# A gate computed token block by token block, and a planner with other costs, in a two-block transformer kernel

## The chip, the cores and the metric

The kernel runs on one core of one Trainium2 chip. Its time is the device time of one execution in microseconds. Three runs of the kernel before took 1854.78, 1855.92 and 1857.61 us; the median is 1855.92 us.

## What is computed

Two blocks on x of 512 tokens by 1024 features, all in float32. The first has two layers; in each, after an attention mixer, comes this (reference, cut):

```python
for i in range(2):
    m = _even_mixer(x, ...) if i % 2 == 0 else _odd_mixer(x, ...)
    x = _layer_norm(DN_ALPHA * x + m, ln1_g[i], ln1_b[i])
    x = _layer_norm(DN_ALPHA * x + _sq_relu_mlp(x, w_up[i], w_down[i]), ln2_g[i], ln2_b[i])
    gate = jax.nn.sigmoid(x @ ple_w_gate[i] + ple_b_gate[i])
    x = x + gate * (p[i] @ ple_w_proj[i])
```

`ple_w_gate[i]` is 1024x1024, `ple_w_proj[i]` 256x1024. The even mixer is latent attention beside sliding-window attention, the odd one attention with forget gates. The second block is `h = rmsnorm(x) @ w_in`, gated linear attention beside a short convolution, an output product, `rmsnorm`, a SiLU feed-forward part and a last `rmsnorm`.

## The kernel before, in words

**Numbers and tiles.** Every float32 matrix is split into a high and a low part (ACT casts the high part, L273; DVE subtracts it for the low part, L284), and each product is three matmuls: high by high, high by low, low by high (L245). A stationary operand is 128x128; a moving one has up to 512 columns. The tokens are four blocks t of 128, the 1024 output columns two halves h of 512. So one half of one token block of the gate is 8 x 3 = 24 matmuls of 128x512, and the whole gate 8 x 24 = 192; the projection p @ w_proj is 8 x 6 = 48.

**Weights.** SP loads a raw unit of 128x1024 (512 KB; L314) into a buffer of the pool `af_t`, ACT casts it, DVE subtracts, and the parts lie in `ar_t`. The gate's weight is eight such units, ("ga", i, h, u) with h the column half and u = 0..3; the projection's is two, ("pr", i, h). A matrix held in one half serves all four token blocks, and its units come free after the last of them.

**From one stage to the next.** A token block of x lies with tokens on partitions; as an operand it is wanted transposed. `to_T` (L631) does this by eight 128x128 transposes on PE (L254, four to a PSUM bank), a cast per bank on ACT and a subtraction per bank on DVE. What stands ahead of it is a chain over four engines. After the MLP it is `ln_finish` (L685): ACT sums the block's halves (`half_sum`, L678), GpSimd makes the mean (L692), ACT squares with accumulation, DVE subtracts and multiplies by g (first of two 128x1024 `scalar_tensor_tensor`, L298), GpSimd makes 1/sqrt in two small steps (`rsqrt`, L621 and L622), DVE scales and adds b (the second). After the gate of layer 1 it is `rms_T` (L737): Square on ACT, two small GpSimd steps, two `scalar_tensor_tensor` of 128x512, then `to_T`.

**The gate** (L1605). First the 48 projection matmuls, whose results ACT copies to SBUF (`keep`). Then for h, for t: 24 matmuls, then `ev_` (L1612): DVE adds the bias, ACT takes the sigmoid, DVE multiplies by the projection and adds to x. When the second half of a block is done, `post` starts: `to_T` after layer 0's gate, `rms_T` after layer 1's. Since h is the outer loop, all four `post` chains start in the second pass.

**What sets the order.** The program is written by generators that yield what they need; `Core.run` (L431) advances the one whose next operation can begin first by a model of the engines' clocks, in which each operation has a cost: a matmul at L235 to L245, a DVE operation in `vcost` (L275), a small GpSimd step where it is issued (L621, L622, L692). The order so made is the fixed program of each engine, which the chip carries out in order. A cost therefore changes no work, only where it stands, and which buffer it gets.

Of the kernel before, what the change touches and what calls it, by code (L numbers as in the profile page):

```python
# [13 lines left out]
ALU = mybir.AluOpType  # L14
# [3 lines left out]
D = 1024  # L18
NB = 4
# [9 lines left out]
class Arena:  # L29


    def __init__(self, ap, n, grain=G):
        self.grain, self.n = grain, 0
        self.used, self.wt, self.rd, self.segs = [], [], [], []
        self.shut = False
        self.add(ap, n)
# [107 lines left out]
class Core:  # L144


    def __init__(self, nc, ar, af, sm, ps):
        self.nc, self.ar, self.af, self.ps = nc, ar, af, ps
        self.clk = dict(pe=0.0, act=0.0, dve=0.0, pool=0.0, dma=0.0)
        self.bw = [0.0] * 8  # L150
        self.br = [0.0] * 8
        self.bfree = [True] * 8
        self.byname = {}
        for x in (ar, af, sm):
            self.names(x)
        self.psname = ps.tensor.name
        self.streams = []
        self.table = None

    def names(self, a):  # L160
        for base, g, ap in a.segs:
            self.byname[ap.tensor.name] = (a, base, g * a.grain)
# [73 lines left out]
    def mm(self, out, lhsT, rhs, start, stop, more=False):  # L236
        n = self.size(rhs)
        slow = 4 if rhs.dtype == F32 else 1
        m = self.size(lhsT)
        if rhs.dtype == F32R:  # L240
            cost = max((n + 32) / 2.4, 109 * m / 128)
        else:
            cost = slow * max(n / 2.39, 107 * m / (256 if rhs.dtype == BF16 else 128))
        self.op("pe", cost, [lhsT, rhs], [out])
        self.nc.tensor.matmul(out, lhsT, rhs, start=start, stop=stop, **(dict(skip_group_check=True) if more else {}))  # L245
# [27 lines left out]
        self.nc.scalar.copy(out, src)  # L273

    def vcost(self, n, fast):  # L275
        return n * (0.53 if fast else 1.042) + (66 if fast else 157)

    def tt(self, out, a, b, op, eng="dve"):
        if eng == "pool":
# [274 lines left out]
def model_kernel(ctx: ExitStack, tc: tile.TileContext, a: dict, dbg=None):  # L554
# [14 lines left out]
    c = Core(nc, R, F, Arena(sm_t, NS, 4), ps_t)  # L569
    xb = [F.take(D, 0) for _ in range(NB)]  # L570
    xt = [b.ap for b in xb]
# [26 lines left out]
    mhalf = cp.tile([P, 4], F32, name="mhalf")  # L598
# [12 lines left out]
    def hs(h):  # L611
        return slice(h * 512, h * 512 + 512)
# [5 lines left out]

    def rsqrt(src, n, scale, eps):
        v, r = small(n), small(n)  # L620
        c.pool(165, [src], [v]).tensor_scalar(out=v, in0=src, scalar1=scale, scalar2=eps, op0=ALU.mult, op1=ALU.add)  # L621
        c.pool(465 + 160 * (n - 1), [v], [r]).tensor_tensor(out=r, in0=v, in1=mhalf[:, :n], op=ALU.pow)  # L622
        return r

    def dump(name):
# [61 lines left out]
    def ln_finish(t, st, g, b, ev):  # L687
        m, v = small(1), small(1)
        tmp = yield from c.alloc(F, D)
        z = yield from c.alloc(F, D)  # L690
        yield ("x", [st])
        c.pool(400, [st], [m]).tensor_scalar(out=m, in0=st[:, 0:1], scalar1=st[:, 1:2], scalar2=-1.0 / D, op0=ALU.add, op1=ALU.mult)  # L692
        yield ("x", [m])
        c.act(z.ap, xt[t], AF.Square, bias=m, accum_out=v)
        c.stt(tmp.ap, xt[t], m, g, ALU.add, ALU.mult)
        z.free()
        r = rsqrt(v, 1, 1.0 / D, EPS1)
        yield ("x", [r])
        c.stt(xt[t], tmp.ap, r, b, ALU.mult, ALU.add)
        tmp.free()  # L700
        yield from to_T(t, xt[t], A["x"], 8, ev)
# [35 lines left out]
    def rms_T(t, g, dst, ev):  # L737
        ss = small(1)
        y = yield from c.alloc(F, D)
        c.act(y.ap, xt[t], AF.Square, accum_out=ss)  # L740
        r = rsqrt(ss, 1, 1.0 / D, EPS2)
        for h in range(2):
            c.stt(y.ap[:, hs(h)], xt[t][:, hs(h)], r, g[:, hs(h)], ALU.mult, ALU.mult)
        yield from to_T(t, y.ap, dst, 8, ev)
        y.free()

# [867 lines left out]
    def gate(i, pT, post):  # L1614
# [24 lines left out]
        def keep(b, z):  # L1639
            yield ("x", [c.pb(b)])  # L1640
            c.acopy(z.ap, c.pb(b))
            c.give(b)

        bps = {}
        for h in range(2):
            for t in range(NB):
                z = bps[h, t] = yield from c.alloc(F, 512)
                b = yield from tm(xcols(pT["x"], range(2), t), [("pr", i, h)], 512, [pT["ev"][t]], t == 3)
                c.spawn(keep(b, z), 0)
        for h in range(2):  # L1650
            keys = [("ga", i, h, u) for u in range(4)]
            for t in range(NB):
                bb = yield from tm(xcols(A["x"], range(8), t), keys, 512, [old[t]], t == 3)
                c.spawn(ev_(bb, bps[h, t], t, h), 0)
        for z in pT["b"]:
# [691 lines left out]
    def main():  # L2347
        yield from new_A()
        for t in range(NB):
            c.spawn(to_T(t, xt[t], A["x"], 8, A["ev"][t]), 0)  # L2350
        W.cap = 4
        yield from layer1()
        yield from mlp(0, pT := {})
        yield from gate(0, pT, lambda t, e: to_T(t, xt[t], A["x"], 8, e))
        W.cap = 4
        yield from layer2()
        yield from mlp(1, pT := {})
        n1 = yield from bcast(a["norm1_g_2"], D)
        yield from gate(1, pT, lambda t, e: rms_T(t, n1.ap, A["x"], e))
        W.cap = 5  # L2360

        def later(ev):
            yield ("x", list(ev))
            n1.free()

        c.spawn(later(A["ev"]), 0)
        yield from layer3()
        yield from ffn()
# [116 lines left out]
```

## Time and profile before

| | |
|---|---|
| profiled execution | 1856.44 us |
| span of its trace | 1854.7 us, so 1.74 us lie outside it |
| median of the runs | 1855.92 us |
| PE (matmuls) busy | 1815.6 us, 98% |
| DVE busy | 1169.7 us, 63% |
| ACT busy | 902.7 us, 49% |
| GpSimd (POOL) busy | 134.2 us, 7% |
| granted TensorE clock, mean of the span | 0.992 |

Read it by PE: 1854.7 less 1815.6 is 39.1 us in which PE does no matmul, in a few places; anywhere else a shorter step on another engine moves nothing. Granted clock is a share of full speed: 1.0 is 2.4 GHz, 0.5 is 1.2 GHz, and a figure between them is a stretch that was partly at each.

### The profile page before, as it was taken

What the parts mean: (1) busy time and instruction counts of PE and PEld (TensorE: products, weight loads), DVE (VectorE), ACT (ScalarE), POOL (GpSimd) and SP (SyncE); (2) the same over time, 40 slices, a digit from 0 to 9 for tenths busy, and PEclk for the clock granted to TensorE, in tenths of its full rate; (3) what the DMA queues carried; (4) which work ended last, traced back from release to release, by engine and by line L of the source; (5) the groups of instructions that cost most, each with busy time, mean ns of one, the idle gap of its engine ahead of it and who ended that gap; (6) DMA issues with size and microseconds to landing.
All of it is one profiled execution on the core that took longest, in us unless ns stands there. A gap on an engine that the chain in (4) does not pass through costs nothing. (4 is left out here: it accounts for less than half of the span.)

```text
span 1854.7 us, 23845 instructions
## 1 busy us (share of the span) xinstructions
PE 1815.6 (98%) x9096; PEld 1518.9 (82%) x9096; DVE 1169.7 (63%) x1947; ACT 902.7 (49%) x1594; POOL 134.2 (7%) x227
## 2 busy tenths in 40 slices
PE   8999999999998999999999999989999999999997
PEld 7876788888887888878888888878889898888886
DVE  4667667566568578778675656675675554644646
ACT  4567464545456365555645454563543243423434
POOL 1000011001011000000110010110010000100001
PEclk9999999999999999999999999999999999999999
DMA  5211256464562122323564736531222443633614
GB/s 171 82 36 47 91 182 163 105 188 85 176 151 89 46 92 69 114 69 114 171 159 112 192 71 193 126 109 65 69 91 75 141 172 103 158 124 80 171 23 97
DMA packets 63539, 212.01 MB, mean 114 GB/s; under 512 B 7544, under 2 KB 10160, under 8 KB 63424
## 3 DMA queue, kind: packets, MB, share of 16 engines
q1 hardware_dynamic: 50752, 165.39, 25.9%
q0 software_dynamic: 12672, 45.09, 14.0%
q8 instruction: 71, 1.16, 0.3%
q14 instruction: 44, 0.36, 0.1%
HBM read 208.32 MB, written 2.14 MB: 113 GB/s over the span
## 5 line engine op out<-in xcount | busy, mean ns | idle before, releaser
L245 PE MATMUL ps_t<-ar_t 128*128 128x512 f32 (+4 forms) x6591 | 1385.6, 367 | 9.4 <-DVE ar_t L293 3.3
L245 PEld LDWEIGHTS ps_t<-ar_t 128*128 128x128 f32 x6591 | 1140.7, 190 | 207.6 <-ACT ar_t L273 7.4
L284 DVE TENSOR_TENSOR ar_t<-af_t,ar_t 128x1024 fp32r<-128x1024 f32 (+5 forms) x456 | 467.5, 1043 | 365.0 <-ACT ar_t L273 361.4
L273 ACT CAST ar_t<-af_t 128x1024 fp32r<-128x1024 f32 (+5 forms) x467 | 412.2, 900 | 495.0 <-PE ps_t L245 325.8
L245 PE MATMUL ps_t<-ar_t,ax_r 128*128 128x512 f32 (+1 forms) x1050 | 258.2, 390 | 2.7 <-ACT ar_t L273 1.8
L245 PEld LDWEIGHTS ps_t<-ar_t,ax_r 128*128 128x128 f32 x1050 | 196.4, 190 | 43.6 <-ACT ar_t L273 2.2
L284 DVE TENSOR_TENSOR ar_t<-ps_t,ar_t 128x512 fp32r<-128x512 f32 (+3 forms) x207 | 117.0, 595 | 94.1 <-ACT ar_t L273 93.3
L273 ACT CAST ar_t<-ps_t 128x512 fp32r<-128x512 f32 (+3 forms) x207 | 98.8, 519 | 139.8 <-PE ps_t L254 70.0
L298 DVE SCALAR_TENSOR_TENSOR af_t<-af_t,ps_t 128x512 f32<-128x512 f32 (+2 forms) x218 | 138.2, 658 | 44.7 <-PE ps_t L245 38.7
L269 ACT ACTIVATE af_t<-af_t 128x512 f32<-128x512 f32 (+3 forms) x144 | 92.3, 644 | 103.9 <-DVE af_t L298 57.1
L284 DVE TENSOR_TENSOR ax_r<-af_t,ax_r 128x256 fp32r<-128x256 f32 (+5 forms) x119 | 91.7, 771 | 59.9 <-ACT ax_r L273 59.3
L273 ACT CAST ax_r<-af_t 128x256 fp32r<-128x256 f32 (+5 forms) x119 | 81.3, 687 | 81.4 <-PE ps_t L245 42.9
L284 DVE TENSOR_TENSOR af_t<-af_t 128x256 f32<-128x256 f32 (+2 forms) x228 | 99.5, 467 | 11.2 <-ACT af_t L269 8.4
L322 POOL DMA_DIRECT2D af_t<-in_w_down x64 | 55.5, 868 | 550.4 <-DVE ar_t L284 525.3
L254 PE MATMUL ps_t<-ident,af_t 128*128 128x128 f32 (+1 forms) x499 | 70.5, 279 | 14.1 <-DVE af_t L298 13.9
L273 ACT COPY af_t<-ps_t 128x512 f32<-128x512 f32 (+3 forms) x108 | 59.1, 569 | 46.6 <-PE ps_t L245 32.6
L254 PEld LDWEIGHTS ps_t<-ident,af_t 128*128 128x128 f32 (+1 forms) x499 | 59.4, 142 | 22.0 <-DVE af_t L298 15.7
L269 ACT ACTIVATE af_t<-af_t,sm_t 128x256 f32<-128x256 f32 (+4 forms) x92 | 60.6, 660 | 30.3 <-DVE sm_t L808 20.9
L245 PE MATMUL ps_t<-ax_r,ar_t 128*128 128x512 f32 (+4 forms) x343 | 70.3, 346 | 0.0
L298 DVE SCALAR_TENSOR_TENSOR af_t<-af_t,sm_t 128x1024 f32<-128x1024 f32 (+1 forms) x48 | 52.1, 1103 | 25.6 <-POOL sm_t L622 12.0
L269 ACT ACTIVATE af_t<-ps_t 128x512 f32<-128x512 f32 (+3 forms) x111 | 58.7, 529 | 15.5 <-PE ps_t L245 15.4
L245 PEld LDWEIGHTS ps_t<-ax_r,ar_t 128*128 128x128 f32 (+1 forms) x343 | 56.6, 186 | 8.3
(98 smaller groups left out, 670.1 us busy)
## 6 DMA issues: line engine op xcount, KB each, us to landing
af_t<-in_w_up SPq DMA_DIRECT2D x64, 512.0 KB, 6.0
af_t<-in_w_down POOLq DMA_DIRECT2D x64, 512.0 KB, 5.6
af_t<-in_w_down SPq DMA_DIRECT2D x48, 512.0 KB, 4.8
af_t<-in_w_ffn_gate SPq DMA_DIRECT2D x22, 512.0 KB, 4.5
af_t<-in_w_ffn_up SPq DMA_DIRECT2D x22, 512.0 KB, 4.5
af_t<-in_w_ffn_down POOLq DMA_DIRECT2D x20, 512.0 KB, 5.5
af_t<-in_ple_w_gate SPq DMA_DIRECT2D x16, 512.0 KB, 5.9
af_t<-in_w_ffn_down SPq DMA_DIRECT2D x15, 512.0 KB, 3.4
```

Source lines behind the costliest of these rows:

```text
L245: self.nc.tensor.matmul(out, lhsT, rhs, start=start, stop=stop, **(dict(skip_group_check=True) if more else {}))
L254: self.nc.tensor.transpose(out, src, ident)
L269: self.nc.scalar.activation(out, src, func, **kw)
L273: self.nc.scalar.copy(out, src)
L284: self.nc.vector.tensor_tensor(out, a, b, op=op)
L298: self.nc.vector.scalar_tensor_tensor(out, a, s, b, op0=op0, op1=op1)
L322: self.nc.gpsimd.dma_start(out, src, accum_op=ALU.add)
```

## The change

The planner's costs become three attributes (`tiny`, `two`, `edge`) that have one value while layer 0's attention (`layer1`) is recorded and another from there on. Against before, the small GpSimd steps cost 165 (which was 400 in `ln_finish`) and 465 in the first part and 850 and 1050 after it; a matmul's 32 extra columns and a DVE operation's 157 count as 0 and 66 in the first part and as before after it. `rms_T` issues one `scalar_tensor_tensor` of 128x1024 in place of two of 128x512. The gate's loops change places: t outside, h inside. So all eight weight units are needed within the first token block, and stay until the last; a block's `post` can start when its own two halves are done.

```diff
--- before.py
+++ after.py
@@ -156,6 +156,7 @@
         self.psname = ps.tensor.name
         self.streams = []
         self.table = None
+        self.tiny, self.two, self.edge = (165, 465), 66, 0
 
     def names(self, a):
         for base, g, ap in a.segs:
@@ -238,7 +239,7 @@
         slow = 4 if rhs.dtype == F32 else 1
         m = self.size(lhsT)
         if rhs.dtype == F32R:
-            cost = max((n + 32) / 2.4, 109 * m / 128)
+            cost = max((n + self.edge) / 2.4, 107 * m / 128)
         else:
             cost = slow * max(n / 2.39, 107 * m / (256 if rhs.dtype == BF16 else 128))
         self.op("pe", cost, [lhsT, rhs], [out])
@@ -273,7 +274,7 @@
         self.nc.scalar.copy(out, src)
 
     def vcost(self, n, fast):
-        return n * (0.53 if fast else 1.042) + (66 if fast else 157)
+        return n * (0.53 if fast else 1.042) + (66 if fast else self.two)
 
     def tt(self, out, a, b, op, eng="dve"):
         if eng == "pool":
@@ -618,8 +619,8 @@
 
     def rsqrt(src, n, scale, eps):
         v, r = small(n), small(n)
-        c.pool(165, [src], [v]).tensor_scalar(out=v, in0=src, scalar1=scale, scalar2=eps, op0=ALU.mult, op1=ALU.add)
-        c.pool(465 + 160 * (n - 1), [v], [r]).tensor_tensor(out=r, in0=v, in1=mhalf[:, :n], op=ALU.pow)
+        c.pool(c.tiny[0], [src], [v]).tensor_scalar(out=v, in0=src, scalar1=scale, scalar2=eps, op0=ALU.mult, op1=ALU.add)
+        c.pool(c.tiny[1] + 160 * (n - 1), [v], [r]).tensor_tensor(out=r, in0=v, in1=mhalf[:, :n], op=ALU.pow)
         return r
 
     def dump(name):
@@ -689,7 +690,7 @@
         tmp = yield from c.alloc(F, D)
         z = yield from c.alloc(F, D)
         yield ("x", [st])
-        c.pool(400, [st], [m]).tensor_scalar(out=m, in0=st[:, 0:1], scalar1=st[:, 1:2], scalar2=-1.0 / D, op0=ALU.add, op1=ALU.mult)
+        c.pool(c.tiny[0], [st], [m]).tensor_scalar(out=m, in0=st[:, 0:1], scalar1=st[:, 1:2], scalar2=-1.0 / D, op0=ALU.add, op1=ALU.mult)
         yield ("x", [m])
         c.act(z.ap, xt[t], AF.Square, bias=m, accum_out=v)
         c.stt(tmp.ap, xt[t], m, g, ALU.add, ALU.mult)
@@ -739,8 +740,7 @@
         y = yield from c.alloc(F, D)
         c.act(y.ap, xt[t], AF.Square, accum_out=ss)
         r = rsqrt(ss, 1, 1.0 / D, EPS2)
-        for h in range(2):
-            c.stt(y.ap[:, hs(h)], xt[t][:, hs(h)], r, g[:, hs(h)], ALU.mult, ALU.mult)
+        c.stt(y.ap, xt[t], r, g, ALU.mult, ALU.mult)
         yield from to_T(t, y.ap, dst, 8, ev)
         y.free()
 
@@ -1647,9 +1647,9 @@
                 z = bps[h, t] = yield from c.alloc(F, 512)
                 b = yield from tm(xcols(pT["x"], range(2), t), [("pr", i, h)], 512, [pT["ev"][t]], t == 3)
                 c.spawn(keep(b, z), 0)
-        for h in range(2):
-            keys = [("ga", i, h, u) for u in range(4)]
-            for t in range(NB):
+        for t in range(NB):
+            for h in range(2):
+                keys = [("ga", i, h, u) for u in range(4)]
                 bb = yield from tm(xcols(A["x"], range(8), t), keys, 512, [old[t]], t == 3)
                 c.spawn(ev_(bb, bps[h, t], t, h), 0)
         for z in pT["b"]:
@@ -2350,6 +2350,7 @@
             c.spawn(to_T(t, xt[t], A["x"], 8, A["ev"][t]), 0)
         W.cap = 4
         yield from layer1()
+        c.tiny, c.two, c.edge = (850, 1050), 157, 32
         yield from mlp(0, pT := {})
         yield from gate(0, pT, lambda t, e: to_T(t, xt[t], A["x"], 8, e))
         W.cap = 4
```

The same instructions are issued as before but for `rms_T`. PE's, DVE's and ACT's order differs in layer 0's attention, in the norm after it, at the end of each MLP with the gate behind it, in the norm after the second attention, and at the beginning and the end of the second block's mixer; inside the MLPs, the second attention, the feed-forward part and the end it is the same. On SP the fifth of the last six gate-weight loads moves ahead of the load of the gate's bias, so that seven of eight stand ahead of it and one behind (six and two before), in both layers.

**PE, end of the first MLP.** The transposes with `ident,af_t ... x8` are T(0) to T(3) of the norm after the MLP. Before:

```order
L245 MATMUL ps_t<-ar_t,ax_r 128x512 x45
L254 MATMUL ps_t<-ident,af_t 128x128 x8
L245 MATMUL ps_t<-ar_t,ax_r 128x512 x15
L254 MATMUL ps_t<-ident,af_t 128x128 x8
L245 MATMUL ps_t<-ar_t,ax_r 128x512 x12
L245 MATMUL ps_t<-ar_t 128x512 x18
L254 MATMUL ps_t<-ident,af_t 128x128 x8
L245 MATMUL ps_t<-ar_t 128x512 x24
L254 MATMUL ps_t<-ident,af_t 128x128 x8
```

Now:

```order
L246 MATMUL ps_t<-ar_t,ax_r 128x512 x13
L255 MATMUL ps_t<-ident,af_t 128x128 x8
L246 MATMUL ps_t<-ar_t,ax_r 128x512 x18
L255 MATMUL ps_t<-ident,af_t 128x128 x8
L246 MATMUL ps_t<-ar_t,ax_r 128x512 x30
L255 MATMUL ps_t<-ident,af_t 128x128 x8
L246 MATMUL ps_t<-ar_t,ax_r 128x512 x12
L246 MATMUL ps_t<-ar_t 128x512 x6
L255 MATMUL ps_t<-ident,af_t 128x128 x8
```

Counting the `ar_t,ax_r` and `ar_t` rows ahead together, T(0) stands 15 matmuls later in the program than it did, and there are 18, 30 and 18 matmuls between the four, where there were 15, 30 and 24. The second MLP's end has the same steps.

**DVE, the same place.** A `af_t,sm_t 128x1024` is a step of `ln_finish`: the first two are block 0's, the next two block 1's. `ar_t<-af_t,ar_t` is the low part of a weight unit, `ps_t 128x512` an addition of the MLP's product to the sum. Before:

```order
L298 SCALAR_TENSOR_TENSOR af_t<-af_t,ps_t 128x512
L298 SCALAR_TENSOR_TENSOR af_t<-af_t,sm_t 128x1024
L298 SCALAR_TENSOR_TENSOR af_t<-af_t,ps_t 128x512
L284 TENSOR_TENSOR ar_t<-af_t,ar_t 128x1024
L298 SCALAR_TENSOR_TENSOR af_t<-af_t,sm_t 128x1024 x2
L298 SCALAR_TENSOR_TENSOR af_t<-af_t,ps_t 128x512 x2
L298 SCALAR_TENSOR_TENSOR af_t<-af_t,sm_t 128x1024
L284 TENSOR_TENSOR ar_t<-ps_t,ar_t 128x4x128 x2
```

Now:

```order
L299 SCALAR_TENSOR_TENSOR af_t<-af_t,ps_t 128x512
L285 TENSOR_TENSOR ar_t<-af_t,ar_t 128x1024
L299 SCALAR_TENSOR_TENSOR af_t<-af_t,sm_t 128x1024
L299 SCALAR_TENSOR_TENSOR af_t<-af_t,ps_t 128x512
L285 TENSOR_TENSOR ar_t<-af_t,ar_t 128x1024
L299 SCALAR_TENSOR_TENSOR af_t<-af_t,ps_t 128x512 x2
L299 SCALAR_TENSOR_TENSOR af_t<-af_t,sm_t 128x1024 x2
L299 SCALAR_TENSOR_TENSOR af_t<-af_t,ps_t 128x512 x3
L299 SCALAR_TENSOR_TENSOR af_t<-af_t,sm_t 128x1024
L285 TENSOR_TENSOR ar_t<-ps_t,ar_t 128x4x128 x2
```

Between block 0's first and second step there stood one addition and one weight unit; now there stand one addition, a weight unit and two more additions, and another weight unit stands ahead of the first.

**PE, end of the gate of layer 1.** The rows with 128x272 are the first product of the second block, 24 for each token block, and need `rms_T` of that block. Before:

```order
L245 MATMUL ps_t<-ar_t 128x512 x30
L254 MATMUL ps_t<-ident,af_t 128x128 x8
L245 MATMUL ps_t<-ar_t 128x512 x12
L245 MATMUL ps_t<-ar_t 128x272 x18
L245 MATMUL ps_t<-ax_r,ar_t 128x272 x6
L245 MATMUL ps_t<-ar_t 128x272 x18
L254 MATMUL ps_t<-ident,af_t 128x128 x4
L245 MATMUL ps_t<-ax_r,ar_t 128x272 x6
L254 MATMUL ps_t<-ident,af_t 128x128 x12
L245 MATMUL ps_t<-ar_t 128x272 x18
L245 MATMUL ps_t<-ax_r,ar_t 128x272 x6
L245 MATMUL ps_t<-ar_t 128x272 x18
```

Now:

```order
L255 MATMUL ps_t<-ident,af_t 128x128 x8
L246 MATMUL ps_t<-ar_t 128x512 x42
L246 MATMUL ps_t<-ar_t 128x272 x6
L255 MATMUL ps_t<-ident,af_t 128x128 x8
L246 MATMUL ps_t<-ar_t 128x272 x12
L246 MATMUL ps_t<-ax_r,ar_t 128x272 x6
L246 MATMUL ps_t<-ar_t 128x272 x18
L246 MATMUL ps_t<-ax_r,ar_t 128x272 x6
L246 MATMUL ps_t<-ar_t 128x272 x18
L246 MATMUL ps_t<-ax_r,ar_t 128x272 x6
L255 MATMUL ps_t<-ident,af_t 128x128 x8
L246 MATMUL ps_t<-ar_t 128x272 x18
```

In the order of before T(3) is the last eight of the row of twelve transposes (the four rows ahead of them and the four further up are T(2)), and stands behind 18 + 6 + 18 + 6 = 48 matmuls of 128x272. Now T(0) has gone ahead into the gate, T(1) and T(2) stand at the top, and T(3) stands behind 6 + 12 + 6 + 18 + 6 + 18 + 6 = 72 of them.

## Rows read from the trace of the kernel before

**Rows 1.** The page's first part: busy us, share of the span, instructions

```profile
PE 1815.6 (98%) x9096; PEld 1518.9 (82%) x9096; DVE 1169.7 (63%) x1947; ACT 902.7 (49%) x1594; POOL 134.2 (7%) x227
```

**Rows 2.** Timeline of PE, first gate's start: start, us, work, idle before

```profile
564.08 1.09 PE L254 MATMUL ps_t<-ident,af_t 128*128 128x128 f32 x8 [3.02 <-DVE af_t L298]
564.92 3.68 PE L245 MATMUL ps_t<-ar_t,ax_r 128*128 128x512 f32 x15
...
574.07 0.50 PE L245 MATMUL ps_t<-ar_t 128*128 128x512 f32 x1 [1.85 <-ACT ar_t L273]
575.33 3.15 PE L245 MATMUL ps_t<-ar_t 128*128 128x512 f32 x8 [0.76 <-DVE ar_t L284]
```

**Rows 3.** Timeline of PE at the second gate's start

```profile
1217.42 1.65 PE L254 MATMUL ps_t<-ident,af_t 128*128 128x128 f32 x8 [2.85 <-DVE af_t L298]
...
1228.98 0.50 PE L245 MATMUL ps_t<-ar_t,ax_r 128*128 128x512 f32 x1 [1.78 <-ACT ar_t L273]
1230.24 4.04 PE L245 MATMUL ps_t<-ar_t,ax_r 128*128 128x512 f32 x11 [0.76 <-DVE ar_t L284]
```

**Rows 4.** Windows: length; busy of PE, PEld, DVE, ACT, POOL; clock; DMA

```profile
564.00:570.00 6.00, 5.92 (x34) 5.14 (x35) 6.00 (x10) 2.95 (x8) 1.51 (x2) 1.00 0.00 0
...
576.00:582.00 6.00, 6.00 (x25) 4.86 (x24) 4.62 (x5) 4.35 (x9) 0.59 (x2) 0.72 0.00 0
1218.00:1224.00 6.00, 6.00 (x27) 5.05 (x26) 5.74 (x9) 1.90 (x4) 1.16 (x2) 0.73 0.00 0
...
1230.00:1236.00 6.00, 5.76 (x19) 4.56 (x20) 5.18 (x6) 3.76 (x7) 0.27 (x1) 0.72 0.12 42
...
1302.00:1308.00 6.00, 6.00 (x34) 6.00 (x33) 2.76 (x5) 1.17 (x2) 0.00 (x0) 0.62 0.00 0
```

**Rows 5.** Timeline of DVE at the first gate's start

```profile
562.74 2.48 DVE L298 SCALAR_TENSOR_TENSOR af_t<-af_t,sm_t 128x1024 f32<-128x1024 f32 x2
565.14 1.27 DVE L298 SCALAR_TENSOR_TENSOR af_t<-af_t,ps_t 128x512 f32<-128x512 f32 x2
...
586.39 1.22 DVE L284 TENSOR_TENSOR ar_t<-af_t,ar_t 128x1024 fp32r<-128x1024 f32 x1 [0.20 <-ACT ar_t L273]
```

**Rows 6.** Timeline of SP: the last two loads of the first gate's weight

```profile
587.64 1.76 SPq L314 DMA_DIRECT2D af_t<-in_ple_w_gate  x2
```

**Rows 7.** The page's last part, loads: KB each, median us to landing

```profile
af_t<-in_ple_w_gate SPq DMA_DIRECT2D x16, 512.0 KB, 5.9
```

**Rows 8.** Timeline of POOL in the first gate's norm

```profile
564.31 0.96 POOL L621 TENSOR_SCALAR sm_t<-sm_t 128x1 f32<-128x1 f32 x1 [1.36 <-ACT af_t L269]
```

**Rows 9.** Timeline of PE at the second gate's end

```profile
1292.04 0.91 PE L245 MATMUL ps_t<-ax_r,ar_t 128*128 128x272 f32 x6
...
1295.04 0.60 PE L254 MATMUL ps_t<-ident,af_t 128*128 128x128 f32 x4
...
1301.60 1.97 PE L254 MATMUL ps_t<-ident,af_t 128*128 128x128 f32 x8 [4.77 <-DVE af_t L298]
```

**Rows 10.** Timeline of DVE there

```profile
1292.34 1.42 DVE L298 SCALAR_TENSOR_TENSOR af_t<-af_t,sm_t 128x512 f32<-128x512 f32 x2 [2.19 <-POOL sm_t L622]
...
1294.13 0.69 DVE L284 TENSOR_TENSOR af_t<-ps_t,af_t 128x512 f32<-128x512 f32 x1
...
1300.80 1.42 DVE L298 SCALAR_TENSOR_TENSOR af_t<-af_t,sm_t 128x512 f32<-128x512 f32 x2 [2.13 <-POOL sm_t L622]
```

**Rows 11.** Timeline of PE in the norm after layer 0's attention

```profile
236.40 2.29 PE L245 MATMUL ps_t<-ar_t 128*128 128x256 f32 x17 [1.24 <-DVE ar_t L284]
```

**Rows 12.** Timeline of PE in the norm after the second attention

```profile
890.14 1.09 PE L254 MATMUL ps_t<-ident,af_t 128*128 128x128 f32 x8 [1.50 <-DVE af_t L298]
```

**Rows 13.** Timeline of PE early in layer 0's attention

```profile
24.62 1.10 PE L245 MATMUL ps_t<-af_t,ax_f 128*128 128x512 f32 x2 [1.09 <-DMA af_t<-ed]
```

**Rows 14.** Timeline of PE and DVE where layer 0's query products begin

```profile
74.99 0.55 PE L254 MATMUL ps_t<-ident,af_t 128*128 128x128 f32 x3 [1.80 <-DVE af_t L298]
...
77.03 1.23 DVE L284 TENSOR_TENSOR ar_t<-af_t,ar_t 128x1024 fp32r<-128x1024 f32 x1 [0.27 <-ACT ar_t L273]
```

## The prediction

> **What bounds the kernel now.** The first part of the page comes first: PE is busy for 1815.6 us of the span [rows 1], and no other engine comes near. PE carries out its program in order, so the time is PE's work and the holes in it; DVE, ACT and GpSimd matter only where PE stands at an instruction whose operand is late. The list of what PE waited for leads to the places, and the timeline of PE shows each of them.
>
> At the start of the first gate PE reaches T(0) of the norm too early: it waits 3.02 us for DVE's last step, and later 1.85 and 0.76 us for the projection's weight, whose cast and subtraction stand late [rows 2]. In the stretch from 576 to 582 us the granted clock is 0.72 of 2.4 GHz, so part of it runs at 1.2 GHz [rows 4]; 0.28 x 6 = 1.7 us go there. Together 7.3 us. The second gate's start repeats it: 2.85, 1.78 and 0.76 us [rows 3], and two stretches at 0.73 and 0.72 [rows 4], 3.3 us: 8.7 us. At the second gate's end PE waits 4.77 us at T(3) [rows 9], and the stretch behind it has a clock of 0.62 [rows 4], 2.3 us more: 7.1 us. These three are 23.1 us. The norm after layer 0's attention has one wait of 1.24 us [rows 11], the one after the second attention 1.50 [rows 12], layer 0's attention 1.09 for a transfer [rows 13] and 1.80 at a transpose [rows 14]. The rest of PE's idle time, at the very start, at the end and in the second attention, lies where the order is the same.
>
> **The change part by part, in order of size.**
>
> Second gate's end. In the program of before the last product of the gate is followed by 48 matmuls of 128x272 and then T(3). Twenty-four of these take 3.0 us (1292.04 to 1295.04) [rows 9], so one takes 0.125, and the gate's last product ended 18 x 0.125 = 2.25 us ahead of the row at 1292.04, at 1289.8. Its addition on DVE came only at 1294.13, because the scaling of block 2 stood ahead and waited for GpSimd until 1292.34 [rows 10]: all four chains ran in the gate's second pass, close behind each other. In the new order a block's chain starts 48 matmuls after the one before, not 24, and those of blocks 0 to 2 are done before block 3's product ends. From the addition at 1294.13 to the scaling step at 1300.80 is 6.67 us, and one step of 128x1024 takes 1.24 (two take 2.48) [rows 5] where the two of 128x512 took 1.42. With the addition at 1290.0 it is done at 1290.0 + 6.7 + 1.2 = 1297.9. PE was at T(3) at 1301.60 - 4.77 = 1296.8 and now has 24 more matmuls ahead of it, so arrives at 1299.8. The wait goes, and so does the slow stretch behind it. What is late next is the product of block 3 itself, which now comes straight behind T(3) where another block's product lay between: one cast and one subtraction of a 128x512 tile, near 0.6 us each by DVE's 1.27 for two [rows 5]. I take 1.2 us for it. Gain 7.1 - 1.2 = 5.9; bounds 7.1, and 3.0 if the chain is no faster than before and only the 24 matmuls help.
>
> The merged scaling step costs DVE less, but T can no longer begin on its first half: 0.6 us later, in the margin of 1.9 us.
>
> Here the Trainium skill bears (GPSIMD Engine Reference, section Key points): GpSimd shares its SBUF interfaces with VectorE, and DVE instructions with two SBUF inputs contend with it. The trace agrees: one small step took 0.96 us beside a double-length DVE step [rows 8]. By the rule the longer scaling step holds a neighbour's small steps back by up to 0.6 us more; where no margin is left that is 0.6 us less gain, and since the blocks now lie 48 matmuls apart, the sum by the rule and mine are the same to 0.6.
>
> Second gate's start. T(0) stands 15 matmuls later, and 15 such matmuls take at most 3.68 us [rows 2]; I take 3.6. But on DVE one weight unit, the projection's (1.22), and two additions (1.27) [rows 5] have come between the first and the second step of block 0's norm, 2.5 us. The wait is 2.85 + 2.5 - 3.6 = 1.75 us in place of 2.85. The two waits for the projection's weight go, since this unit is what has come forward. For that the gate's units are late next: eight are wanted within the first block's 48 matmuls, 11.5 us at 3.6 / 15 = 0.24 each, where four were wanted there and four in the second pass, and DVE is already busy for all of 564 to 570 us [rows 4]. Eight by 1.22 is 9.8 us of DVE; several have been done by the time PE comes, and I take 0.5 us of small waits. The clock: it stayed at 1.00 behind the wait of 3.02 us and fell behind that of 2.85 [rows 2 to 4], so I count one stretch at half weight, 0.85 us. Left 1.75 + 0.5 + 0.85 = 3.1 of 8.7: gain 5.6, bounds 0 and 8.7.
>
> [...]
>
> First gate's start. The same steps: 3.02 + 2.5 - 3.6 = 1.9, with 0.5 and 0.85 makes 3.25 of 7.3: gain 4.1, bounds 0 and 7.3. Its end has no wait in either order, since T there waits for no norm.
>
> Norm after layer 0's attention. T(1) stands 6 matmuls earlier, and its two subtractions on DVE earlier with it, so the low parts that PE waited 1.24 us for are there: gain 1.2, bounds 0 and 1.2. In the norm after the second attention the wait of 1.50 us [rows 12] moves to the next product: nothing, bounds 0 and 1.5.
>
> Layer 0's attention. Six matmuls and two groups of transposes now stand ahead of the one that waits 1.09 us for a transfer [rows 13]: gain 1.0. Where the query products begin, the low part of a value-weight unit, 1.23 us [rows 14], comes ahead of the latent's low parts on DVE, and PE already stands there: loss 1.3. Net loss 0.3; bounds 2.9 better (both waits of rows 13 and 14 gone) and 2.5 worse (two such units).
>
> Second block's mixer and the norm behind it. No wait there before; the new order puts the norm's steps ahead of a feed-forward weight unit. I take one unit late, 1.2 us; bounds 0 and 2.5.
>
> The sum: 5.9 + 5.6 + 4.1 + 1.2 - 0.3 - 1.2 = 15.3 us. The profiled execution took 1856.44 us (the span and 1.74 us outside it), so 1841.1; it lay 0.5 above the median of the runs, so the forecast is **1841 us** (0.1 between the two is nothing). Its own range is 1834 to 1847.
>
> **The rivals.**
>
> *The gate starts keep their loss.* DVE is the second bound there: it was busy for the whole of 564 to 570 us [rows 4], and the new order asks more of it earlier. If the waits of T(0) only turn into waits for the gate's units, the 9.7 us of both starts stay and 15.3 - 9.7 = 5.6 is left: 1850.8. For it: a unit serves 6 matmuls, 1.44 us, and costs DVE 1.22, which leaves almost no room for the norm's own steps. Against: several units are subtracted before PE is there. Chance 0.20.
>
> *All of it.* T(0) is on time, no unit is late, the clock stays up: 3.1 + 3.25 more, 1834.8. For it: the same places lost nothing else before. Against: the sum of DVE's rows. Chance 0.15.
>
> *Slower: the eighth unit.* Two loads of the gate's weight were issued only at 587.64 us [rows 6], when buffers came free, and 5.9 us is a usual landing [rows 7]; in the new order one of them is still behind the bias load and is needed at the end of the first block, not in the second pass. Issued at 587.64 it is landed at 593.5 and, with a cast and a subtraction of about 1.2 us each, ready at 596. PE is done waiting at T(0) at 561.1 + 3.6 + 1.9 = 566.6, and has 102 matmuls and four groups of transposes at 0.84 (564.08 to 564.92) [rows 2] until it wants it: 566.6 + 24.5 + 3.4 = 594.5, so it would be 1.5 us late. It decides when it slips by a whole buffer turn: the gain of 15.3 is gone when both gates lose 7.7 us to it, and a slip of 10 us each gives 1841 + 20 = 1861. For it: nothing lets SP pass a waiting load. Against: its buffer is freed by the second unit, which is split early. Chance 0.06.
>
> *Near nothing.* Both starts keep their loss, layer 0 loses 2.5 instead of 0.3 and the mixer 2.5 instead of 1.2: 1850.8 + 3.5 = 1854.3. Chance 0.09.
>
> **How the numbers follow.** The forecast has 0.50. The range reaches from all of it with layer 0 better, 1832, to the gate starts keeping their loss with one more unit late, 1852; outside lie near nothing, slower, and a little at the lower end, under 0.2. Within 0.2% (3.7 us, about what a measurement of this kernel can tell from no change) is near nothing, 0.09; slower 0.06; faster 0.85.
>
> **What would show it.** In the new profile T(3) at the second gate's end begins without a wait and the clock stays at 1.00 there; T(0) at each start still waits for DVE, some 2 us, and no wait for the cast of the projection's weight is left; small waits for DVE stand in the gate's first 48 matmuls and none in the later ones; the wait of 1.24 us is gone; layer 0 is as long as before to 2 us. I am wrong in the gates if waits of several us for a weight's load or subtraction stand in the first block, and in layer 0 or the mixer if the stretches 0 to 230 or 1290 to 1510 us of before take over 3 us more.

## The result and the profile after

The changed kernel takes 1842.74 us (median of 4 runs, 1841.28 to 1842.99), the kernel before 1856.57 (4 runs); the ratio is 0.9925, with a 95% interval of 0.9908 to 0.9942. It is 13.8 us faster; forecast were 1841 us and a gain of 15.3, with a range of 1832 to 1852. The profiled execution took 1841.28 us, its span is 1839.6 us; it is the fastest of the four, 1.5 us under the median, so the places below add up to 15.1 us and not to 13.8. The page's first part [rows 1]:

```profile
PE 1810.7 (98%) x9096; PEld 1514.0 (82%) x9096; DVE 1165.8 (63%) x1939; ACT 901.0 (49%) x1594; POOL 141.3 (8%) x227
```
and the main lines of what PE waited for (us in total, times, longest), two of before and then those of the changed kernel:

```profile
PE ps_t L254 <- DVE af_t L298: 13.9, 5, 4.8
PE ps_t L245 <- ACT ar_t L273: 4.8, 4, 1.9
```
```profile
PE ps_t L255 <- DVE af_t L299: 6.9, 3, 3.0
...
PE ps_t L246 <- DVE ar_t L285: 3.1, 5, 0.8
PE ps_t L246 <- ACT ar_t L274: 2.6, 4, 1.1
...
PE ps_t L246 <- DMA af_t<-ed: 0.5, 1, 0.5
```

PE was idle for 28.9 us of the span (1839.6 less 1810.7), 39.1 before, and busy for 4.9 us less with the same matmuls, at a mean clock of 0.996 in place of 0.992. The waits for DVE's steps at L299 (L298 before) have gone from 13.9 us in five to 6.9 in three, those for a cast on ACT from 4.8 to 2.6. Where the difference was made is read at points that both programs pass with the same work behind them:

| the same point in both programs | before | after | ahead by |
|---|---|---|---|
| a product in layer 0's attention | 170.93 | 170.56 | 0.4 |
| a late product of the second attention | 712.37 | 707.99 | 4.4 |
| second MLP, transposes of p | 1144.84 | 1140.46 | 4.4 |
| behind the second gate (16-wide transposes) | 1313.56 | 1297.30 | 16.3 |
| inside the second block's mixer | 1392.50 | 1376.47 | 16.0 |
| end of the span | 1854.7 | 1839.6 | 15.1 |

The transposes of p in the first MLP stand at 489.97 and 489.56 us, with 6 matmuls (1.4 us) more ahead of them now: 1.8 us ahead there. So layer 0 with its norm gave 1.8 us, the first gate 2.6, the second gate's start and end 11.9, and the mixer took 1.1 back.

The timeline of PE where the first gate begins [rows 2]:

```profile
565.66 1.97 PE L255 MATMUL ps_t<-ident,af_t 128*128 128x128 f32 x8 [2.98 <-DVE af_t L299]
567.28 5.11 PE L246 MATMUL ps_t<-ar_t,ax_r 128*128 128x512 f32 x18
572.23 1.03 PE L255 MATMUL ps_t<-ident,af_t 128*128 128x128 f32 x8
573.02 7.07 PE L246 MATMUL ps_t<-ar_t,ax_r 128*128 128x512 f32 x30
579.92 1.04 PE L255 MATMUL ps_t<-ident,af_t 128*128 128x128 f32 x8
580.72 3.01 PE L246 MATMUL ps_t<-ar_t,ax_r 128*128 128x512 f32 x12
583.56 1.53 PE L246 MATMUL ps_t<-ar_t 128*128 128x512 f32 x6
584.93 1.03 PE L255 MATMUL ps_t<-ident,af_t 128*128 128x128 f32 x8
```

T(0) still waits, for 2.98 us, and its transposes and the 18 products behind it run slowly; T(1) to T(3) and the gate's products have no wait, and none is left for the projection's unit. At the second gate's start [rows 3]:

```profile
1215.76 1.09 PE L255 MATMUL ps_t<-ident,af_t 128*128 128x128 f32 x8 [2.17 <-DVE af_t L299]
1216.61 4.38 PE L246 MATMUL ps_t<-ar_t,ax_r 128*128 128x512 f32 x18
...
1238.59 3.72 PE L246 MATMUL ps_t<-ar_t 128*128 128x512 f32 x15 [0.68 <-DVE ar_t L285]
```

and at its end [rows 9]:

```profile
1288.94 0.91 PE L246 MATMUL ps_t<-ax_r,ar_t 128*128 128x272 f32 x6
1289.69 1.03 PE L255 MATMUL ps_t<-ident,af_t 128*128 128x128 f32 x8
1290.97 0.52 PE L246 MATMUL ps_t<-ar_t 128*128 128x272 f32 x2 [0.24 <-ACT ar_t L274]
1291.69 2.27 PE L246 MATMUL ps_t<-ar_t 128*128 128x272 f32 x16 [0.21 <-DVE ar_t L285]
```

The wait of 4.77 us is gone: T(3) follows the product ahead of it at once, and 0.24 + 0.21 us remain for its own cast and subtraction. The windows of these places, with the clock in the last column but two [rows 4]:

```profile
564.00:570.00 6.00, 4.34 (x17) 3.82 (x18) 6.00 (x8) 4.16 (x11) 2.76 (x3) 0.72 0.00 0
...
1212.00:1218.00 6.00, 3.83 (x22) 3.00 (x21) 6.00 (x8) 3.66 (x8) 3.04 (x4) 1.00 0.15 59
1218.00:1224.00 6.00, 6.00 (x33) 5.02 (x32) 6.00 (x9) 5.59 (x12) 1.52 (x3) 1.00 0.36 121
1290.00:1296.00 6.00, 5.55 (x38) 4.84 (x37) 4.79 (x9) 3.61 (x6) 0.00 (x0) 1.00 0.22 68
```

None of the four slow stretches of before [rows 4] stands where it stood; a new one has come behind the first T(0), where the clock was 1.00 before. The norm after layer 0's attention has no wait; the one after the second attention keeps 1.26 of 1.50 us [rows 12], at the product behind T(1):

```profile
884.69 0.38 PE L246 MATMUL ps_t<-ar_t 128*128 128x256 f32 x1 [0.47 <-ACT ar_t L274]
885.86 2.29 PE L246 MATMUL ps_t<-ar_t 128*128 128x256 f32 x17 [0.79 <-DVE ar_t L285]
```

In layer 0's attention the transfer's wait is down to 0.54 us, and where the query products begin [rows 14] three waits add up to 3.78 us (before: the 1.80 of the transposes and 0.79 behind them):

```profile
73.46 0.55 PE L255 MATMUL ps_t<-ident,af_t 128*128 128x128 f32 x3 [1.79 <-DVE af_t L299]
75.15 0.50 PE L246 MATMUL ps_t<-ar_t 128*128 128x512 f32 x1 [1.14 <-ACT ar_t L274]
76.50 3.94 PE L246 MATMUL ps_t<-ar_t 128*128 128x512 f32 x10 [0.85 <-DVE ar_t L285]
```

### The profile page after: what moved, and what is told of

The parts are those of the page before. It is cut to its first block, busy times and chain, and to the rows that moved or that the text cites. A ratio compares the mean times of both kernels' runs of the same rounds, so it can differ in the third digit from the quotient of the medians.

```text
span 1839.6 us, 23837 instructions
## 1 busy us (share of the span) xinstructions
PE 1810.7 (98%) x9096; PEld 1514.0 (82%) x9096; DVE 1165.8 (63%) x1939; ACT 901.0 (49%) x1594; POOL 141.3 (8%) x227
## 5 line engine op out<-in xcount | busy, mean ns | idle before, releaser
L285 DVE TENSOR_TENSOR ar_t<-af_t,ar_t 128x1024 fp32r<-128x1024 f32 (+4 forms) x450 | 457.6, 1034 | 356.1 <-ACT ar_t L274 353.4
L274 ACT CAST ar_t<-af_t 128x1024 fp32r<-128x1024 f32 (+4 forms) x477 | 412.1, 884 | 489.2 <-PE ps_t L246 329.1
L246 PE MATMUL ps_t<-ar_t,ax_r 128*128 128x512 f32 (+3 forms) x979 | 252.2, 387 | 0.4 <-ACT ax_r L274 0.2
L246 PEld LDWEIGHTS ps_t<-ar_t,ax_r 128*128 128x128 f32 (+1 forms) x979 | 180.4, 188 | 37.4 <-issue 1.0
L299 DVE SCALAR_TENSOR_TENSOR af_t<-af_t,ps_t 128x512 f32<-128x512 f32 (+2 forms) x218 | 138.1, 659 | 43.9 <-PE ps_t L246 37.8
L285 DVE TENSOR_TENSOR ar_t<-ps_t,ar_t 128x512 fp32r<-128x512 f32 (+4 forms) x181 | 104.3, 602 | 82.6 <-ACT ar_t L274 81.3
L274 ACT CAST ar_t<-ps_t 128x512 fp32r<-128x512 f32 (+4 forms) x181 | 88.4, 525 | 111.9 <-PE ps_t L246 48.7
L285 DVE TENSOR_TENSOR ax_r<-af_t,ax_r 128x1024 fp32r<-128x1024 f32 (+4 forms) x109 | 90.9, 834 | 69.4 <-ACT ax_r L274 68.9
L274 ACT CAST ax_r<-af_t 128x1024 fp32r<-128x1024 f32 (+4 forms) x109 | 80.1, 738 | 86.4 <-PE ps_t L246 55.5
L323 POOL DMA_DIRECT2D af_t<-in_w_down x64 | 55.4, 866 | 551.5 <-DVE ar_t L285 531.1
L246 PE MATMUL ps_t<-ax_r,ar_t 128*128 128x512 f32 (+5 forms) x451 | 97.0, 352 | 0.0
L299 DVE SCALAR_TENSOR_TENSOR af_t<-af_t,sm_t 128x1024 f32<-128x1024 f32 x40 | 51.0, 1279 | 20.3 <-POOL sm_t L623 17.5
```

Source lines behind the costliest of these rows:

```text
L285: self.nc.vector.tensor_tensor(out, a, b, op=op)
L299: self.nc.vector.scalar_tensor_tensor(out, a, s, b, op0=op0, op1=op1)
L323: self.nc.gpsimd.dma_start(out, src, accum_op=ALU.add)
```

## The experiments

Ten kernels were run, each four to eleven times, beside the kernel before. "Before" is 1855.76, 1856.20 and 1856.53 us in the three sessions; each ratio is to that of its own session.

**The gate's loops alone.** The kernel before with

```diff
-        for h in range(2):
-            keys = [("ga", i, h, u) for u in range(4)]
-            for t in range(NB):
+        for t in range(NB):
+            for h in range(2):
+                keys = [("ga", i, h, u) for u in range(4)]
```

> The kernel before with the gate's loops exchanged and nothing else. Theory (the places add up, each part of the change owns some): the second gate's end loses its wait of 4.77 us at T(3) and the slow clock behind it, since that comes from the spacing of the blocks; the two starts keep their waits at T(0), 3.0 and 2.9 us, and the two later waits for the projection's weight, since those come from the planner's costs of the small steps. Gain 5 to 7 us, near 1850. Rival (the loop only pays together with the costs): with all eight units wanted in the first block and the projection's unit still late, the starts get worse by what the end gains; 1855 to 1858.

Measured: 1849.61 us, ratio 0.9962 (0.9949 to 0.9976), 6.2 us gained. PE's timeline at the second gate's end has no wait; T(3) is the two groups of four transposes:

```profile
1300.60 2.04 PE L245 MATMUL ps_t<-ar_t 128*128 128x272 f32 x15
1302.47 0.60 PE L254 MATMUL ps_t<-ident,af_t 128*128 128x128 f32 x4
1302.83 0.62 PE L245 MATMUL ps_t<-ar_t 128*128 128x272 f32 x3
1303.29 0.60 PE L254 MATMUL ps_t<-ident,af_t 128*128 128x128 f32 x4
```

while T(0) waited 4.02 and 3.07 us at the two starts and the two waits for the projection's unit (1.80 and 0.76) stood there as before. The theory holds: the spacing of the blocks owns the end. The wait at the first T(0), 1.0 us longer in a program in which PE's order up to there was not changed, was not expected.

**The costs of the small steps alone.** The kernel before with these two, and 400 kept for `ln_finish` in layer 0's attention:

```diff
-        c.pool(165, [src], [v])...
+        c.pool(c.tiny[0], [src], [v])...
...
         yield from layer1()
+        c.tiny = (850, 1050)
```

> The kernel before with only the cost of the small GpSimd steps raised to 850 and 1050 behind layer 0's attention. Theory: T(0) moves 15 matmuls later at both starts and the projection's unit comes forward, so both starts gain as in the changed kernel, 2.6 and 6 us; the second gate's end keeps its wait near 4.8 us and its slow clock; the second block's mixer loses about 1. Gain 6 to 8 us, near 1849. Rival (costs that are too high only make PE wait elsewhere): within 2 us of before.

Measured: 1845.66 us, ratio 0.9949 (0.9937 to 0.9961), 10.1 us: more than expected. T(0) waited only 1.72 and 1.42 us, with the clock at 1.00 behind both, and the end kept its wait:

```profile
1283.14 1.27 PE L255 MATMUL ps_t<-ident,af_t 128*128 128x128 f32 x8
1288.38 1.84 PE L255 MATMUL ps_t<-ident,af_t 128*128 128x128 f32 x8 [3.96 <-DVE af_t L299]
1289.87 3.62 PE L246 MATMUL ps_t<-ar_t 128*128 128x272 f32 x18
```

So this part owns the starts; T(0) waited 1.3 and 0.8 us less than in the changed kernel, with the same position on PE.

**The costs inside layer 0's attention alone.** `two` and `edge` 66 and 0 there, 165 in `ln_finish`, and the costs of before behind it.

> The kernel before with only the costs inside layer 0's attention changed. Theory: the transfer wait of 1.09 us and the norm's wait of 1.24 us go, as in the changed kernel (0.4 us by 170 us of the span, 1.8 behind the norm): gain 1 to 2 us, 1854 to 1855.5, every later place as before. Rival: the places behind it shift in time and the gate's starts or their clock change with them: more than 3 us either way.

Measured: 1856.57 us (11 runs), ratio 1.0004 (0.9995 to 1.0012, or 0.9 us faster to 2.2 slower): nothing, where 1 to 2 us were expected. The norm's wait of 1.24 us was gone, but the three waits at the query products came to 3.9 us and the stretch from 78 to 84 us ran at a clock of 0.54.

**The changed kernel with the loops of before.** The loop edit above, taken back.

> The changed kernel with the gate's loops as before. Theory: the second gate's end has its wait of about 4 us at T(3) and the slow clock back, 5.5 us; T(0)'s waits at the starts are 1.7 and 1.4 as with the small steps alone, and not 3.0 and 2.2, and no slow stretch follows them, 3 us less; near 1845. Rival (the longer waits at T(0) belong to the planner's costs together, not to the loop): 1847.5 to 1849.

Measured: 1846.43 us, ratio 0.9946 (0.9933 to 0.9958). The time lies between the theory's 1845 and the rival's 1847.5, and the theory's reason fell: T(0) waited 3.10 and 3.33 us, so the long waits do not belong to the new loop. The end was better than with the small steps alone: two waits of 1.71 and 2.24 us in place of one of 3.96, with the clock at 1.00 behind them.

**The changed kernel with the costs of before in layer 0's attention.**

> The changed kernel with the costs of before inside layer 0's attention. Theory (what the new order saves there in waits, 1.24 us in the norm and about 1 for the transfer, it gives back where the query products begin, in waits and clock): within 1 us of the changed kernel, 1842 to 1844. Rival (the 1.8 us that the changed kernel's trace is ahead behind that norm are its gain): 1844.5.

Measured: 1842.78 us, ratio 0.9925 (0.9913 to 0.9937), the changed kernel's own ratio. With the run on that part alone: these costs are worth nothing that can be measured.

**The scaling step in halves again.** `rms_T` as before in the changed kernel.

> The changed kernel with the scaling step in two halves of 128x512 again. Theory: the wide step has a margin at the second gate's end, so nothing is gained or lost by it: 1842.7 within 1 us, and T(3) there begins with no wait over 0.5 us either way. Rival (the wide step frees DVE and GpSimd at the right moment and carries part of the gain): 2 us or more slower than the changed kernel.

Measured: 1843.00 us, ratio 0.9934 (0.9922 to 0.9947); at the second gate's end T(3) starts without a wait and its first products wait 0.24 and 0.21 us, as in the changed kernel. The wide step is worth nothing that can be measured. On DVE's timeline, with block 3's last addition above it, it ended at 1287.86 + 1.28 = 1289.1 us in the changed kernel, 0.55 ahead of T(3):

```profile
1279.97 0.69 DVE L285 TENSOR_TENSOR af_t<-ps_t,af_t 128x512 f32<-128x512 f32 x1
...
1287.86 1.28 DVE L299 SCALAR_TENSOR_TENSOR af_t<-af_t,sm_t 128x1024 f32<-128x1024 f32 x1 [2.13 <-POOL sm_t L623]
```

**What T(0) waits for.** Ahead of block 0's norm stands a chain: the last two units of the down weights, (y, 0) and (y, 1), are completed by a transfer each that GpSimd issues (L323) and that adds to what lies in their buffer; ACT casts the first of them, DVE subtracts, adds the MLP's sums behind it, and only then can block 0's norm begin. In the changed kernel GpSimd issued the two transfers at 543.19 and 544.33 us, and ACT waited until 553.77 for the first. The timeline of GpSimd's queue there:

```profile
543.19 0.86 POOL L323 DMA_DIRECT2D af_t<-in_w_down  x1 [4.79 <-DVE ar_t L285]
544.33 0.87 POOL L323 DMA_DIRECT2D af_t<-in_w_down  x1 [0.27 <-issue]
```
and the timeline of ACT, with the cast of (y, 0) and, at 557.37, the first operation of block 0's norm:

```profile
553.77 1.05 ACT L274 CAST ar_t<-af_t 128x1024 fp32r<-128x1024 f32 x1 [4.57 <-DMA af_t<-in_w_down]
...
557.37 0.63 ACT L270 ACTIVATE af_t<-af_t 128x512 f32<-128x512 f32 x1 [2.07 <-DVE af_t L299]
```

Which of the two the cast waited for is told by the view of transfers, with KB and us from issue to landing, for the issue at 543.19 and for the one at 544.33:

```profile
af_t<-in_w_down POOLq DMA_DIRECT2D x1, 512.0 KB, 10.6
af_t<-in_w_down POOLq DMA_DIRECT2D x1, 512.0 KB, 13.2
```

543.19 + 10.6 is 553.8, where the cast begins; the second landed only at 557.5. The expectations of the runs below pair this cast with the issue at 544.33, and L is counted so here: the time from the second issue to the cast, 9.44 us. The second issue follows the first by 1.13 or 1.14 us in every program, so L is the first transfer's time less that, and differences between programs are the same. First and second start:

| program | L | wait at T(0) | L less the wait |
|---|---|---|---|
| before | 8.56, 8.37 | 3.02, 2.85 | 5.54, 5.52 |
| loops alone | 9.56, 8.61 | 4.02, 3.07 | 5.54, 5.54 |
| layer 0's costs alone | 8.52, 8.40 | 2.99, 2.87 | 5.53, 5.53 |
| small steps alone | 8.17, 7.87 | 1.72, 1.42 | 6.45, 6.45 |
| changed kernel | 9.44, 8.62 | 2.98, 2.17 | 6.46, 6.45 |
| with the old loops | 9.56, 9.79 | 3.10, 3.33 | 6.46, 6.46 |
| with layer 0's old costs | 8.64, 8.47 | 2.18, 2.02 | 6.46, 6.45 |
| with halves | 9.53, 8.74 | 3.07, 2.28 | 6.46, 6.46 |

(The runs with the gate loads held, below, have 6.51 or 6.52 at four starts.) The last column has two values, one for each order. So the wait moves one to one with this transfer's time, less what the order lets lie beside it; the new order lets 0.92 us more.

**The gate's later loads held back.** In the changed kernel SP issued three gate loads between 545.09 and 547 us, beside these transfers. Here (diff cut) the third load takes the buffer of the down unit (y, 0), so that it and the loads behind it go out after that unit's split, in the trace at 555.42 us; PE's order is unchanged.

```diff
+            if key[0] == "ga" and key[2:] == (0, 2):
+                yield ("x", [lambda: bool(self.held)])
+                raw = self.held.pop()
...
+        if key[0] == "dn" and key[2:] == (3, "y", 0):
+            self.held.append(raw)
+            return
```

> The changed kernel, in which the third to eighth load of the gate's weight go out only when the first of the last down units (y, 0) has been split: the third takes that unit's buffer, the others stand behind it on SP. PE's order is that of the changed kernel. Theory (T(0) is late because the last accumulating load of the down weight, issued at 544.33 us in the changed kernel's trace and cast at 553.77, shares the DMA engines with three gate loads issued from 545.09 on): the cast comes at least 2 us earlier after its issue (9.4 us before), T(0)'s waits of 2.98 and 2.17 us shrink to under 1, the clock stays up behind them; 1836 to 1840. Rival (T(0) is late by DVE's order alone, as the prediction worked it out): waits as they are, or longer for later gate units, 1842 or slower.

Measured: 1839.09 us, ratio 0.9906 (0.9893 to 0.9919). L is 8.17 and 7.26 us, the wait at T(0) 1.66 and 0.75, and the clock stayed at 1.00. The issue on GpSimd's timeline:

```profile
544.91 0.87 POOL L323 DMA_DIRECT2D af_t<-in_w_down  x1 [0.27 <-issue]
```

the cast on ACT's:

```profile
553.08 1.05 ACT L274 CAST ar_t<-af_t 128x1024 fp32r<-128x1024 f32 x1 [3.66 <-DMA af_t<-in_w_down]
```

T(0) on PE's:

```profile
564.93 1.09 PE L255 MATMUL ps_t<-ident,af_t 128*128 128x128 f32 x8 [1.66 <-DVE af_t L299]
565.78 4.37 PE L246 MATMUL ps_t<-ar_t,ax_r 128*128 128x512 f32 x18
```

and the window of that place:

```profile
564.00:570.00 6.00, 5.07 (x27) 4.29 (x28) 6.00 (x8) 4.22 (x10) 2.79 (x3) 1.00 0.03 14
```

The transfer that the cast waited for, issued at 543.78, took 9.3 us to land and not 10.6, in the view of transfers:

```profile
af_t<-in_w_down POOLq DMA_DIRECT2D x1, 512.0 KB, 9.3
```

The theory holds for the time and the direction; L fell by 1.3 and 1.4 us and not by 2, and the first wait is not under 1. The time's interval overlaps the changed kernel's (0.9908 to 0.9942), though four of the five runs lie below the fastest of its four. The gate loads are a part of L: it is 7.15 to 8.17 us at the six starts with them held, here and below, and 7.87 to 9.79 at the ten of the new order in the table. They are not all that tells programs apart, since the small steps alone had 8.17 and 7.87 with these loads beside the transfer. What makes the rest, above 7 us with no gate load beside it, was not tried apart; two loads of the norm's vectors (512 KB each, issued at 540.97 and 541.40 us, 7.0 and 8.5 us to landing) and the accumulating load ahead (issued at 538.13, 9.7 us) ran beside it in this trace too.

**The same, with the costs of before in layer 0's attention.**

> The two edits together: the later gate loads held, and the costs of before inside layer 0's attention. If both theories hold, as the run with the loads held alone within 1 us, 1836 to 1840; it shows whether the gain at T(0) stands in another program too.

Measured: 1842.61 us, ratio 0.9921 (0.9908 to 0.9934), against the expectation, and no different from the run with these costs and no load held (1842.78). T(0) waited 0.76 and 0.81 us with L at 7.28 and 7.32, so that part stands in another program; but the first gate waited 0.38 and 0.76 us for a unit of its weight, and the profiled execution ran slower between 6 and 12 us and at the query products. Of the 5.6 us by which its span is longer than that of the run with the loads alone held (1841.7 and 1836.1), 3.8 lie ahead of the transposes of p in the first MLP (492.56 us, against 490.14 there with 6 matmuls more ahead), before any load is held. So the unit that came late explains 1.1 us at most, and that holding the loads shortens the whole run is shown with one set of layer 0's costs and not with the other.

**The projection's units split later.** They wait until the norm of block 0 has had its last step on DVE (`c.lns` counts these steps):

```diff
+            if key[0] == "pr":
+                yield ("x", [lambda: c.lns >= 8 * key[1] + 5])
...
+        c.lns += 1
```

> The changed kernel, in which the projection's two weight units are not split before the norm of block 0 has had its last step on DVE; the planner then sets T(0) 6 matmuls earlier at both starts. So far T(0)'s wait at the 13 starts traced with the small steps' new costs is L - 6.45 us, L being the time from the issue of the last accumulating down load to its cast on ACT. Theory (that constant is the arithmetic of PE's and DVE's order, as the prediction used it): one unit less on DVE makes T(0) ready 1.15 us earlier, 6 matmuls less bring PE there 1.36 us earlier, so the wait is L - 6.24 within 0.1; and the projection's unit is late again, with waits of 1 to 2 us for it; 1843 to 1846. Rival (the constant is an accident of load times and not of the order): off by 0.5 us or more.

Measured: 1842.91 us, ratio 0.9931 (0.9918 to 0.9945). L is 9.13 and 8.40 us and the waits are 2.90 and 2.16: L less 6.23 and 6.24, as worked out from the order beforehand. The clock stayed at 1.00 behind the wait of 2.90 us and fell behind that of 2.16 (0.85 and 0.87 from 1212 to 1224 us). The projection's unit was less late than expected, 0.49 us at the first start and nothing at the second:

```profile
565.94 1.09 PE L255 MATMUL ps_t<-ident,af_t 128*128 128x128 f32 x8 [2.90 <-DVE af_t L299]
...
571.32 1.09 PE L255 MATMUL ps_t<-ident,af_t 128*128 128x128 f32 x8 [0.16 <-DVE af_t L299]
...
573.13 6.89 PE L246 MATMUL ps_t<-ar_t,ax_r 128*128 128x512 f32 x29 [0.49 <-DVE ar_t L285]
```

**T(0) later, with the loads held.** In the planner, block 0 waits 2500 more before its transposes:

```diff
+        if t == 0 and c.two == 157:
+            yield ("x", [c.clk["dve"] + 2500.0])
         yield from to_T(t, xt[t], A["x"], 8, ev)
```

> The kernel with the later gate loads held, and block 0's transposes held back in the planner, which sets T(0) 6 matmuls later at both starts. Theory: the wait at T(0) is L - 6.45 - 1.36; with an L of 7.3 to 8.2 as in the runs with the loads held that is 0 to 0.4 us, and nothing else moves: 1 to 2 us below that kernel, 1837 to 1838.5. Rival (the waits are only handed on to T(1), which now stands 20 matmuls behind T(0) and not 26, or to the units of the gate): 1839 or more.

Measured: 1838.33 us (1837.64 to 1838.47), ratio 0.9902 (0.9889 to 0.9916), the fastest of all and all four runs below the changed kernel's, though only 0.8 us below the run with the loads alone held, with overlapping intervals. L was 8.07 and 7.15; T(0) waited 0.19 us and nothing, against 0.26 and nothing by the rule. But 0.34 us came up at T(1) of the first start and 0.60 at a later one of the second: part was handed on.

```profile
564.76 1.09 PE L255 MATMUL ps_t<-ident,af_t 128*128 128x128 f32 x8 [0.19 <-DVE af_t L299]
565.61 3.00 PE L246 MATMUL ps_t<-ar_t,ax_r 128*128 128x512 f32 x12
568.95 1.09 PE L255 MATMUL ps_t<-ident,af_t 128*128 128x128 f32 x8 [0.34 <-DVE af_t L299]
```

## Why the prediction was right, and where not

*What bounds the kernel.* Right: of the 15.1 us of the profile 10.2 are holes in PE's work, and 4.9 are PE's busy time for the same matmuls, at a higher mean clock.

*Second gate's end, 5.9.* Right. T(3) has no wait, and 0.45 us for its cast and subtraction stands where 1.2 was taken. The loops alone gave 6.2 us. The margin of the wide step was 0.55 us and not 1.9: from block 3's last addition (1279.97) to the scaling step (1287.86) are 7.89 us, where 6.67 were taken. The rule of the Trainium skill (GPSIMD Engine Reference, section Key points) on the interfaces that GpSimd shares with VectorE agrees with one small step of 1.48 us beside two DVE steps of 128x1024 in the first gate's norm (row below, GpSimd's timeline; 0.55 is the usual). Nothing hangs on it at the second gate's end, where the time is the same with the scaling step in halves.

```profile
565.74 1.48 POOL L623 TENSOR_TENSOR sm_t<-sm_t,mhalf 128x1 f32<-128x1 f32 x1
```

*Second gate's start, 5.6.* Right: T(0) waited 2.17 us (1.75 taken), small waits 0.68 (0.5), and the waits for the projection's unit are gone. That no slow stretch came, where half of one was counted, is luck in part: one came behind the 2.16 us of the run with the projection's units later. Start and end together gave 11.9 us, where 11.5 were forecast.

*First gate's start, 4.1.* 2.6 was measured. The step that failed is "3.02 + 2.5 - 3.6 = 1.9": its two terms for the order were nearly right (1.1 us better taken, 0.92 measured at equal L), but 3.02 was used as a constant, and it moves with the time of the accumulating load of (y, 0), with an L of 9.44 us in the changed kernel's profile and 8.56 in the one before. So 2.98 us came where 1.9 was taken. Beside that, a whole slow stretch came where half of one was counted, 0.85 us worse, and none of the small waits, 0.5 better.

*The norms.* 1.2 and nothing forecast; the first wait is gone, the second is 1.26 of 1.50.

*Layer 0's attention, -0.3.* The two runs on its costs hold the first norm's 1.2 as well: 0.9 better was forecast for both together, and no difference was measured. The trace of the changed kernel is 1.8 us ahead behind that norm, 0.4 of it inside the attention, but single executions differ by more, through the clock from 6 to 18 us of the span. So no time is shown to be gained here, though the norm's wait is gone.

*Mixer, -1.2.* 1.1 were lost, but not as reasoned: no wait for a feed-forward unit appears. Most of it, 0.9, lies between 1376 us and the end, spread over products that have no wait but one of 0.23 us; what makes it was not tried.

*The rivals.* "The gate starts keep their loss" fell: with the small steps alone the starts gave more than half of the whole gain; "near nothing" fell with it. "The eighth unit" fell: the load went out at 585.21 us and no wait for it followed. "All of it" did not happen; with the loads held and T(0) set later, 1838.3 was reached.

*The sum of the parts.* Loops alone 6.2, small steps alone 10.1, layer 0 alone -0.8: 15.5, where together they gave 13.8. The difference fits T(0)'s L in these programs (8.2 with the small steps alone, 9.4 with all); that this is its cause is not shown, as every program has one profile. And that the profile's 15.1 meets the 15.3 forecast is partly luck: 1.5 too little at the first gate is made up by 0.9 too much in layer 0 and its norm, which the runs on its costs do not confirm, and by 0.4 at the second gate.

## What to carry to other kernels

A wait that a profile shows at one engine for another can be a transfer several steps up the chain: compare the wait with that transfer's duration over several programs, and a difference that stays constant tells what belongs to the order and what to the load. Which transfer it is must be read from its landing, since two that are always issued one behind the other fit equally well. Costs alone did most here: with the small steps at 850 and 1050 in the planner's model it set T(0) 15 matmuls later, and the run with that alone gained 10.1 us. When loops are exchanged so that blocks finish evenly, the chains behind them stop queueing on the engine they share; here this was worth 6.2 us, and making one scaling step of two nothing that can be measured. Loads issued early for a later stage can slow a load that the present stage waits for (10.6 us to landing with them, 9.3 without); held back, they can come late in their own turn (0.38 and 0.76 us).

## What had not been expected of the hardware

The accumulating load of 512 KB that T(0)'s chain waits for had an L of 7.15 to 9.79 us in the twelve programs traced, 8.3 to 10.9 us from its own issue, and L differed between the two layers of one program by up to 0.95 us. A wait of T(0) near 3 us was followed by a slow stretch in some executions (0.72 of 2.4 GHz behind 2.98 us) and by none in others (1.00 behind 3.02 us [rows 2, 4]), and so was a shorter one: the clock stayed at 1.00 behind 2.17 us in the changed kernel and fell behind 2.16 us with the projection's units later. The stretch from 6 to 12 us of the span ran at 0.72 to 0.82 in five of the ten profiled executions of the experiments and shows 1.00 in the others; by an estimate from these figures (0.18 to 0.28 of 6 us) that alone moves a run by 1.1 to 1.7 us.
